# Which matmuls of two fused transformer blocks carry an order edge inside the attentions

## The chip, the cores and the metric

The kernel runs on one core of one Trainium2 chip. The metric is device time in microseconds (us), first instruction to last, as the median of three executions. The core's engines are called PE (TensorE matmul), PEld (its weight load, which overlaps PE), DVE (VectorE), ACT (ScalarE), POOL (GpSimd) and SP (SyncE, which issues most of the DMAs).

## What is computed

Two blocks follow each other on 1024 positions of width 1024, with 256 context positions beside them. The first block has two layers. Each projects its normed input to 28 tiles of 128 columns and mixes them in four ways: a short convolution, a grouped-query attention (GQA, 4 heads of 64 on 2 key heads), a gated scan (HGRN) and a Fourier mix.

```
def hybrid_layer(h, hc, ...):
    shift, scale, gate = jnp.split((c_act @ w_mod + b_mod)[:, None, :], 3, axis=-1)
    lat = split_cols((rms_norm(h, norm_g) * (1.0 + scale) + shift) @ w_in)
    att_l, att_c = gqa_branch(lat[4], lat[5], lat[6], cx[4], cx[5], cx[6], q_g, k_g, cos, sin, need_ctx)
    hg_l, hg_c = hgrn_branch(...)
    y_conv, y_four, g_att, g_hg = mix_stream(lat, conv_w)
    y = jnp.concatenate([y_conv, att_l * g_att, hg_l * g_hg, y_four], axis=-1) @ w_out
    h_new = h + gate * y
```

The second block has a latent attention (MLA, 16 heads), a state-space scan (SSD) and a gated feed-forward net. Everything is float32; a product of two float32 operands is made of three matmuls on a high and a low part.

## The kernel before

The kernel is written engine by engine, but not in the order in which the engines run it. Each instruction is traced once, in program order, and a scheduler then sets each engine's order: among the instructions whose inputs its own timing has ready, an engine takes the one that was traced first. So an instruction that is ready early can be taken ahead of others that were traced before it and still wait. An **order edge** from A to B on one engine costs no semaphore; it only tells the scheduler that B stands behind A.

Two streams are woven into each other. The foreground is a mixer (GQA, HGRN, MLA, SSD). The background, `self.lane`, holds the projections: `project` (L375: three matmuls per weight tile, `mm<-xh,wh`, `mm<-xl,wh`, `mm<-xh,wl`, into the three `mm` buffers of PSUM), the spill of each result to DRAM (`sp`), and rows of the modulation (L315, eight matmuls a row). `self.dense(us)` traces some microseconds of the lane at that place in the foreground, so that PE has something to do while the foreground waits for other engines.

The GQA of a layer (`gqa`) works in two halves, one per pair of heads. Each half begins with a prelude: load the queries (`qx`), square sums on PE (L243), their roots on DVE, a spread of the roots by PE transposes (L260), the rotation by `rope` on DVE, the split into high and low parts (`qa`), and the maxima of the first block of scores (matmul L643, reduction L490, transposes L497). Then come the steps: for each block of 512 or 256 queries, `weigh` makes the scores of a key tile (L656 and L657), their exponential (L529) and later the weighted values (L551); the maxima of the next block (`beside`) and the transposes that end the block before (`weigh_end`, L574 and L581) are traced within these steps, and so is `self.dense(wait)`. Scores, maxima and transposes share the three `t` buffers of PSUM.

In the kernel before, `weigh` opens `with self.behind(self.last):` around the whole loop over the keys (from L525), around the rest of `beside` (L547) and around the weighted values (L550). `behind` is `issue_after`: every PE instruction traced inside, by whatever it calls, gets an edge behind `self.last`, the transposes of the block's own maxima. That holds for the scores and for the projections that `dense` traces there. After the GQA follows the HGRN; each of its blocks of 512 positions has eight levels (L865, with operands made on DVE and ACT, and two `copy_predicated` L870 a level), and `dense` traces projections between the levels too, which carry no edge.

Of the kernel before, what the change touches and what calls it, by code (L numbers as in the profile page):

```python
# [15 lines left out]
AF = mybir.ActivationFunctionType  # L16
# [5 lines left out]
P = 128  # L22
# [67 lines left out]
class Kern:  # L90
# [391 lines left out]
    def put_max(self, row, nq, widths, scores):  # L482
# [4 lines left out]
        m = self.tmp("sm", (P, 4, 4), bufs=3)[:, :nq, :k]  # L487
# [8 lines left out]
        for a in range(nq):  # L496
            self.last = self.PE.transpose(t[:, a * P:(a + 1) * P], r[:, a], self.ident)  # L497
        self.S.activation(row, t, AF.Copy)

    def weigh(self, pool, out, keys, n, scores, v, beside, pieces, steps):  # L500
# [23 lines left out]
        done, left = 0, pieces + 1 if beside else 0  # L524
        with self.behind(self.last):  # L525
            for i, j in enumerate(keys):
                s = scores(j)
                e = self.ctmp(pool, "e", (P, 512), ebufs)[:, :n]
                S.activation(e, s, AF.Exp)  # L529
                count(i, e)  # L530
                es.append(e)
                self.dense(wait)
                if i == tail:
                    self.weigh_end()
                while done < left and done * (len(keys) - ahead) < (i + 1) * pieces:
                    done += 1
                    next(beside, None)
            while done < left:
                done += 1
                next(beside, None)  # L540
            self.weigh_end()

        self.last = self.scored
        for i, (j, e) in enumerate(zip(keys, es)):
            h = 64 * (i % 2)
            if i == min(4, len(keys)):
                with self.behind(self.last):  # L547
                    for _ in beside or ():
                        pass
            with self.behind(self.last):  # L550
                self.last = PE.matmul(o[h:h + 64], v(j), e, start=i < 2, stop=i >= len(keys) - 2)  # L551
        for _ in beside or ():
# [6 lines left out]
    def behind(self, ins):  # L559

        return self.tc.issue_after(ins.ins) if ins is not None else nullcontext()

    def weigh_end(self):
# [9 lines left out]
        for a in range(nq):  # L573
            PE.transpose(t[:, a * P:(a + 1) * P], total[:, a * P:(a + 1) * P], self.ident)  # L574
        r = self.tmp("sl", (P, 4), bufs=3)[:, :nq]
# [4 lines left out]
        for a in range(nq):  # L580
            PE.transpose(b[:, a * P:(a + 1) * P], r[:, a:a + 1].to_broadcast([P, P]), self.ident)  # L581
        u = self.tmp("nt")[0:64, :n]
# [46 lines left out]
    def gqa(self, pool, layer, src, need_ctx, y):  # L629
# [7 lines left out]
        def maxima(i, t0, m, h):  # L637
            cols = ALL if t0 < T else CTX

            def scores(a, c):  # L640
                c0, w = cols[c]
                s = self.psum("t")[:, :w]
                self.PE.matmul(s, qs[i][h][:, t0 + a * P:t0 + (a + 1) * P], ks[i][0][:, c0:c0 + w])  # L643
                return s
# [7 lines left out]
        def weigh(i, t0, m, h, b, beside, pieces):  # L652
            def scores(j):
                s = self.psum("t")[:, :m]
                cs = slice(j * P, (j + 1) * P)
                self.PE.matmul(s, ks[i][0][:, cs], qs[i][h][:, t0:t0 + m], start=True, stop=False)  # L656
                self.scored = self.PE.matmul(s, ks[i][1][:, cs], b[:, :m], start=False, stop=True)  # L657
                return s
# [700 lines left out]
    def mla(self, pool, more, kv, done, beside, y):  # L1359
# [39 lines left out]
        def maxima(p, h, t0, m):  # L1399
            def scores(a, c):  # L1400
                c0, w = ALL[c]
                s = self.psum()[:, :w]
                PE.matmul(s, qt[h][:, 0, t0 + a * P:t0 + (a + 1) * P], kt[h][:, 0, c0:c0 + w])  # L1403
                return s
# [3 lines left out]
        def weigh(p, h, t0, m, beside):  # L1408
            def scores(j):
                s = self.psum("t")[:, :m]  # L1410
                kh, kl = (kt[h][:, a, j * P:(j + 1) * P] for a in range(2))
                qh, ql = (qt[h][:, a, t0:t0 + m] for a in range(2))
                PE.matmul(s, kh, qh, start=True, stop=False)  # L1413
                PE.matmul(s, kh, ql, start=False, stop=False)  # L1414
# [698 lines left out]
```

## Time and profile before

| | us |
|---|---|
| median of the runs | 4070.14 |
| lowest and highest of 3 | 4065.42, 4072.88 |
| the profiled execution | 4065.49 |
| its span in the trace | 4063.6 |
| PE busy | 3739.2 (92%) |
| DVE, ACT, POOL busy | 2292.6, 1574.5, 1525.7 |

The span is what the trace shows from the first to the last instruction; 1.9 us lie around it. Matmuls are pipelined, so a matmul's own duration in the trace is longer than the distance from it to the next one. The page also gives the TensorE clock that was granted: full is 2.4 GHz, and half is 1.2 GHz. A table of stretches gives, for each, the busy time of each engine with its count of instructions, the granted clock (1.00 or 0.50 or a mean of the two), the share of the DMA engines and GB/s.

### The profile page before, as it was taken

What the parts mean: (1) busy time and instruction counts of PE and PEld (TensorE: products, weight loads), DVE (VectorE), ACT (ScalarE), POOL (GpSimd) and SP (SyncE); (2) the same over time, 40 slices, a digit from 0 to 9 for tenths busy, and PEclk for the clock granted to TensorE, in tenths of its full rate; (3) what the DMA queues carried; (4) which work ended last, traced back from release to release, by engine and by line L of the source; (5) the groups of instructions that cost most, each with busy time, mean ns of one, the idle gap of its engine ahead of it and who ended that gap; (6) DMA issues with size and microseconds to landing.
All of it is one profiled execution on the core that took longest, in us unless ns stands there. A gap on an engine that the chain in (4) does not pass through costs nothing.

```text
span 4063.6 us, 54946 instructions
## 1 busy us (share of the span) xinstructions
PE 3739.2 (92%) x19642; PEld 2879.9 (71%) x19642; DVE 2292.6 (56%) x4017; ACT 1574.5 (39%) x2851; POOL 1525.7 (38%) x1321
## 2 busy tenths in 40 slices
PE   7978999988979988987999987999999989999998
PEld 4755677767756667666767765666667979988986
DVE  5244486756245487678766776666664474424321
ACT  4223433335323445354434253444443343333332
POOL 2223311026314311255122133556665444445443
PEclk8988999999989999989999999999999999999999
DMA  6531222256532311264344567452223463333232
GB/s 213 166 101 62 88 84 80 89 182 187 187 118 65 109 65 62 78 201 141 130 151 148 184 192 217 108 149 64 51 53 122 156 197 95 98 111 124 92 115 83
DMA packets 274054, 499.54 MB, mean 123 GB/s; under 512 B 31122, under 2 KB 76978, under 8 KB 270772
## 3 DMA queue, kind: packets, MB, share of 16 engines
q1 hardware_dynamic: 269780, 467.06, 36.2%
q0 software_dynamic: 4000, 28.97, 3.0%
q8 instruction: 155, 2.54, 0.3%
q14 instruction: 119, 0.97, 0.1%
HBM read 376.70 MB, written 119.21 MB: 122 GB/s over the span
## 4 chain that ended last, share of the span: by engine, by line
PE 38%; DVE 11%; DMA 3%; issue 2%; ACT 2%; POOL 1%; SPq 0%; DVEq 0%; ACTq 0%; POOLq 0%
PE mm L207 22%; PE mm L375 5%; PE o L551 3%; DVE sm L490 3%; DVE sp L1218 2%; PE mm L1403 1%; PE t L1642 1%; PE o L1620 1%; DVE eb L519 1%; PE t L1577 1%; PE t L1415 1%; PE t L1414 1%; PE t L1413 0%; ACT sw L1610 0%; DVE sp L1215 0%
## 5 line engine op out<-in xcount | busy, mean ns | idle before, releaser
L198 POOL TENSOR_TENSOR wl<-wr,wh 128x512 fp32r<-128x512 f32 (+1 forms) x630 | 849.7, 1355 | 1540.7 <-ACT wh L197 1458.6
L375 PE MATMUL mm<-xh,wh 128*128 128x512 f32 (+1 forms) x1704 | 661.8, 389 | 16.6 <-ACT mrow L323 6.5
L375 PE MATMUL mm<-xh,wl 128*128 128x512 f32 (+1 forms) x1704 | 648.2, 381 | 1.5 <-POOL wl L198 1.5
L375 PE MATMUL mm<-xl,wh 128*128 128x512 f32 (+1 forms) x1704 | 646.7, 380 | 3.0 <-POOL xl L354 1.5
L197 ACT ACTIVATE wh<-wr 128x512 fp32r<-128x512 f32 (+1 forms) x630 | 386.7, 619 | 667.3 <-PE mm L207 253.3
L375 PEld LDWEIGHTS mm<-xh,wh 128*128 128x128 f32 x1704 | 328.5, 193 | 90.5 <-issue 10.5
L529 ACT ACTIVATE e<-t 128x512 f32<-128x512 f32 (+1 forms) x488 | 286.7, 594 | 257.8 <-PE t L1415 122.4
L522 POOL TENSOR_TENSOR ea<-ea,e 128x512 f32<-128x512 f32 x240 | 327.5, 1365 | 134.6 <-ACT e L529 124.7
L375 PEld LDWEIGHTS mm<-xl,wh 128*128 128x128 f32 x1704 | 328.1, 193 | 65.4 <-issue 4.8
L375 PEld LDWEIGHTS mm<-xh,wl 128*128 128x128 f32 x1704 | 328.2, 193 | 65.1 <-issue 6.0
L207 PE MATMUL mm<-fxh,wh 128*128 128x512 f32 (+2 forms) x1056 | 338.6, 322 | 3.2 <-ACT fxh L1794 2.1
L207 PE MATMUL mm<-fxl,wh 128*128 128x512 f32 (+2 forms) x1056 | 337.9, 320 | 1.6 <-DVE fxl L1795 1.6
L207 PE MATMUL mm<-fxh,wl 128*128 128x512 f32 (+2 forms) x1056 | 338.9, 321 | 0.0
L490 DVE TENSOR_REDUCE sm<-mm 128x1 f32<-128x512 f32 (+1 forms) x384 | 207.1, 589 | 14.2 <-PE mm L1403 14.0
L207 PEld LDWEIGHTS mm<-fxl,wh 128*128 128x128 f32 x1056 | 200.3, 190 | 19.0 <-DVE fxl L1795 2.9
L207 PEld LDWEIGHTS mm<-fxh,wh 128*128 128x128 f32 x1056 | 199.9, 190 | 18.8 <-ACT fxh L1794 2.6
L207 PEld LDWEIGHTS mm<-fxh,wl 128*128 128x128 f32 x1056 | 200.3, 190 | 15.2
L519 POOL TENSOR_TENSOR ea<-e 128x512 f32<-128x512 f32 (+1 forms) x52 | 65.3, 1255 | 307.2 <-ACT e L529 300.2
L551 PE MATMUL o<-e,v 128*64 128x512 f32 x640 | 155.5, 602 | 0.0
L375 PE MATMUL mm<-yh,wh 128*128 128x512 f32 (+1 forms) x320 | 124.5, 398 | 26.4 <-ACT yh L994 20.0
L1832 DVE TENSOR_SCALAR fc<-gs,vecs 128x512 f32<-128x512 f32 x44 | 54.8, 1245 | 163.9 <-ACT gs L1828 163.7
L584 DVE TENSOR_TENSOR nt<-o,nt 64x512 f32<-64x512 f32 (+1 forms) x52 | 34.4, 661 | 194.0 <-ACT nt L583 193.8
(466 smaller groups left out, 7890.1 us busy)
## 6 DMA issues: line engine op xcount, KB each, us to landing
mr<-w_mod SPq DMA_DIRECT2D x192, 256.0 KB, 5.2
wr<-w_in SPq DMA_DIRECT2D x190, 256.0 KB, 2.9
wr<-w_up SPq DMA_DIRECT2D x176, 256.0 KB, 2.7
wr<-w_out SPq DMA_DIRECT2D x144, 256.0 KB, 3.2
wr<-w_down SPq DMA_DIRECT2D x80, 256.0 KB, 2.6
q<-qd POOLq DMA_DIRECT2D x16, 768.0 KB, 6.1
rope<-rope SPq DMA_DIRECT2D x20, 512.0 KB, 4.3
k<-kd POOLq DMA_DIRECT2D x16, 640.0 KB, 7.3
```

The lines of the kernel that those rows point to most:

```text
L197: self.S.activation(hi, raw, AF.Copy)
L198: self.G.tensor_tensor(lo, raw, f32(hi), op=ALU.subtract)
L207: self.PE.matmul(out, a, b, start=i == 0, stop=i == n - 1)
L375: self.PE.matmul(ps, a, b, start=at + i == 0, stop=at == k_tiles - 1 and i == 2)
L490: V.tensor_reduce(m[:, a, c:c + 1], scores(a, c), axis=AX.X, op=ALU.max, negate=True)
L519: E.tensor_tensor(total, sums[E][0], e, op=ALU.add)
L522: E.tensor_tensor(sums[E][0], sums[E][0], e, op=ALU.add)
L529: S.activation(e, s, AF.Exp)
L551: self.last = PE.matmul(o[h:h + 64], v(j), e, start=i < 2, stop=i >= len(keys) - 2)
L1218: V.scalar_tensor_tensor(c, u[:, s0 + a:s0 + a + n], cw[:, a:a + 1], c, op0=ALU.mult, op1=ALU.add)
L1403: PE.matmul(s, qt[h][:, 0, t0 + a * P:t0 + (a + 1) * P], kt[h][:, 0, c0:c0 + w])
L1832: V.tensor_scalar(c, gs[:, o:o + 512], w[:, 0:1], b, op0=ALU.mult, op1=ALU.add)
```

## The change

`behind` no longer opens a block: it takes one instruction and gives that one an order edge behind `self.last`. It is called on the first matmul of each score (L643, L656, and L1403, L1413 in the MLA), on the weighted values (L551) and on the transposes of the attention (L497, L574, L581). What `dense` traces within the steps carries no edge any more.

```
     def behind(self, ins):
-        return self.tc.issue_after(ins.ins) if ins is not None else nullcontext()
+        if self.last is not None:
+            how = mybir.DependencyInfo(mybir.DependencyClass.NoSync, mybir.DependencyReason.DATA)
+            self.tc.add_manual_dep(ins.ins, self.last.ins.name, how, reason="order")
+        return ins
...
         for a in range(nq):
-            self.last = self.PE.transpose(t[:, a * P:(a + 1) * P], r[:, a], self.ident)
+            self.last = self.behind(self.PE.transpose(t[:, a * P:(a + 1) * P], r[:, a], self.ident))
...
-        with self.behind(self.last):
-            for i, j in enumerate(keys):
-                s = scores(j)
...
-                self.dense(wait)
+        for i, j in enumerate(keys):
+            s = scores(j)
...
+            self.dense(wait)
...
             if i == min(4, len(keys)):
-                with self.behind(self.last):
-                    for _ in beside or ():
-                        pass
-            with self.behind(self.last):
-                self.last = PE.matmul(o[h:h + 64], v(j), e, start=i < 2, stop=i >= len(keys) - 2)
+                for _ in beside or ():
+                    pass
+            self.last = self.behind(PE.matmul(o[h:h + 64], v(j), e, start=i < 2, stop=i >= len(keys) - 2))
...
-                self.PE.matmul(s, qs[i][h][:, t0 + a * P:t0 + (a + 1) * P], ks[i][0][:, c0:c0 + w])
+                self.behind(self.PE.matmul(s, qs[i][h][:, t0 + a * P:t0 + (a + 1) * P], ks[i][0][:, c0:c0 + w]))
```

The same wrap stands around the transposes of `weigh_end` and the first matmul of the other score functions.

What it does to the order is seen at three places. The instructions are the same ones on every engine; on PE, the rows differ from the square sums of layer 0's first GQA prelude to that layer's HGRN, and from layer 1's GQA to the first matmuls of that layer's output projection. In the MLA and behind it PE's order is unchanged.

The first place is PE in the first prelude of layer 0's GQA (L243 square sums, L260 spread of the roots, L643 maxima, L497 transposes of the maxima, L656 first score). Before, nothing stands between them:

```order
L243 MATMUL t<-bd_70,sq 128x2 x10
L260 MATMUL t<-ident,nt 128x128 x10
L643 MATMUL t<-ka,qa 128x512 x2
...
L497 MATMUL t<-ident,sr 1x128 x4
L656 MATMUL t<-qa,ka 128x512
```

The same place with the change, from the second group of square sums to the first spread:

```order
L243 MATMUL t<-bd_70,sq 128x2 x4
L375 MATMUL mm<-xh,wh 128x256
L375 MATMUL mm<-xl,wh 128x256
L375 MATMUL mm<-xh,wl 128x256
L243 MATMUL t<-bd_70,sq 128x2 x2
...
L315 MATMUL mm<-mr,mact 32x512 x8
L375 MATMUL mm<-xh,wh 128x512
L375 MATMUL mm<-xl,wh 128x512
L260 MATMUL t<-ident,nt 128x128 x4
L375 MATMUL mm<-xh,wl 128x512
```

Projections that stood within the steps now stand between the links of the prelude.

The second place is PE in the first HGRN block of layer 0 (L865 is a level's scores). Before, projections stand between one level and the next:

```order
L865 MATMUL t<-hq,hw 128x128 x8
L375 MATMUL mm<-xh,wh 128x512
L375 MATMUL mm<-xl,wh 128x512
L375 MATMUL mm<-xh,wl 128x512
...
L865 MATMUL t<-hw 128x128 x8
```

With the change the eight levels follow each other, and so do the block's outputs (L885, L888):

```order
L865 MATMUL t<-hq,hw 128x128 x8
L865 MATMUL t<-hw 128x128 x56
L315 MATMUL mm<-mr,mact 32x512
L885 MATMUL t<-sc,hv 64x128
```

The matmuls that stood there have moved to earlier places.

The third place is SP, behind the load of the first queries (`q_0`); `rope` is the rotation table that the prelude's DVE work reads, `mr` and `wr` are raw weights. A piece of the difference:

```order
 L136 DMA qx_1771<-q0_0_1307 128x1280
-L136 DMA rope_1899<-rope1 128x2x512
-L136 DMA rope_2889<-rope1 128x2x512
-L136 DMA qx_2766<-kr_0_1559 64x1280 x2
 L139 DMA hi0_0_1906<-sp_2135 128x512
...
 L136 DMA mr_2409<-w_mod 128x512
+L136 DMA rope_1899<-rope1 128x2x512
 L136 DMA mr_2411<-w_mod 128x512
```

The `rope` load now stands behind a spill of the lane and behind five loads of modulation weights.

## Rows read from the trace of the kernel before

**Rows 1.** The page: the span, the engines' busy time, the granted clock in 40 slices.
```profile
span 4063.6 us, 54946 instructions
...
PE 3739.2 (92%) x19642; PEld 2879.9 (71%) x19642; DVE 2292.6 (56%) x4017; ACT 1574.5 (39%) x2851; POOL 1525.7 (38%) x1321
...
PEclk8988999999989999989999999999999999999999
```
**Rows 2.** Stretches of layer 0: prelude, steps, prelude, steps, three of the HGRN.
```profile
219.00:260.70 41.70, 20.32 (x77) 14.67 (x75) 21.84 (x44) 8.04 (x11) 1.81 (x2) 0.60 0.30 88
260.70:345.80 85.10, 82.84 (x390) 50.65 (x389) 38.42 (x74) 37.66 (x66) 44.51 (x38) 0.97 0.15 48
345.80:387.00 41.20, 32.76 (x161) 24.71 (x159) 22.62 (x46) 9.83 (x16) 7.20 (x7) 0.80 0.40 126
387.00:479.00 92.00, 89.53 (x424) 57.22 (x422) 41.65 (x82) 36.68 (x67) 45.38 (x44) 0.98 0.11 31
...
531.00:562.20 31.20, 30.27 (x216) 23.41 (x215) 30.90 (x70) 8.52 (x15) 2.74 (x2) 1.00 0.09 33
...
583.70:613.70 30.00, 29.33 (x216) 23.02 (x215) 27.10 (x58) 9.92 (x17) 2.56 (x2) 1.00 0.27 92
613.70:635.50 21.80, 21.80 (x141) 16.02 (x140) 12.58 (x34) 3.46 (x7) 3.10 (x3) 1.00 0.10 33
```
**Rows 3.** Stretches of layer 1: prelude, steps, prelude, steps, then the HGRN's end.
```profile
1151.80:1192.20 40.40, 17.44 (x75) 11.39 (x74) 20.66 (x43) 7.54 (x11) 1.79 (x2) 0.59 0.42 133
1192.20:1258.80 66.60, 66.52 (x301) 43.10 (x300) 32.76 (x58) 28.96 (x49) 35.73 (x29) 0.96 0.08 26
1258.80:1300.10 41.30, 33.48 (x150) 21.58 (x148) 23.27 (x45) 10.93 (x17) 10.87 (x9) 0.83 0.34 106
1300.10:1385.30 85.20, 85.13 (x411) 54.44 (x410) 38.33 (x73) 33.65 (x62) 44.33 (x42) 0.98 0.19 59
...
1661.90:1691.20 29.30, 29.30 (x205) 22.36 (x204) 27.98 (x59) 9.53 (x16) 5.38 (x2) 1.00 0.07 28
1691.20:1704.70 13.50, 13.50 (x79) 9.59 (x79) 2.62 (x11) 3.15 (x4) 1.20 (x9) 1.00 0.13 40
1704.70:1749.50 44.80, 34.93 (x117) 23.27 (x115) 16.27 (x24) 18.54 (x34) 15.59 (x12) 0.81 0.68 215
1749.50:1798.80 49.30, 42.74 (x167) 33.33 (x167) 36.83 (x56) 26.22 (x50) 29.43 (x22) 0.86 0.65 204
```
**Rows 4.** PE's longest waits in the first prelude (219 to 260.7): us, times, longest.
```profile
PE t L243 <- ACT sq L461: 6.6, 1, 6.6
PE t L643 <- DVE qa L625: 6.0, 1, 6.0
```
**Rows 5.** Four stretches at half clock, each from a prelude into its steps.
```profile
227.60:265.10 37.50, 18.51 (x57) 13.32 (x58) 20.34 (x42) 7.82 (x10) 0.00 (x0) 0.50 0.21 63
...
377.70:391.40 13.70, 11.28 (x27) 7.41 (x28) 9.86 (x18) 3.36 (x6) 0.00 (x0) 0.50 0.34 111
1159.40:1196.90 37.50, 17.29 (x52) 12.46 (x53) 19.95 (x41) 7.58 (x10) 0.14 (x1) 0.50 0.29 95
...
1289.10:1302.80 13.70, 9.55 (x23) 5.97 (x24) 9.08 (x16) 4.14 (x6) 0.00 (x0) 0.50 0.00 0
```
**Rows 6.** Line 375 alone, 30 matmuls of 512 columns in a row (PE, PEld, clock, DMA).
```profile
1705.03:1712.00 6.97, 6.97 (x30) 5.54 (x30) 1.00 0.47 150
```
**Rows 7.** DVE by line in the first HGRN block: two groups of the lane's convolution.
```profile
L442 DVE SCALAR_TENSOR_TENSOR sp<-cu,vecs,sp 128x512 f32<-128x512 f32 x2 | 1.5, 745 | 0.0
L435 DVE TENSOR_TENSOR cu<-cu,mm 128x512 f32<-128x512 f32 x2 | 1.4, 682 | 0.0
```
**Rows 8.** Line 865 alone in the first HGRN block (PE, PEld, clock, DMA).
```profile
531.00:562.20 31.20, 11.58 (x128) 9.23 (x128) 1.00 0.09 33
```
**Rows 9.** Issues of DMAs: count, KB each, median us from issue to landing.
```profile
mr<-w_mod SPq DMA_DIRECT2D x192, 256.0 KB, 5.2
...
rope<-rope SPq DMA_DIRECT2D x20, 512.0 KB, 4.3
```

More of the change, by code (lines that the diff above doesn't have):

```diff
@@ L1 @@
-from contextlib import ExitStack, nullcontext
+from contextlib import ExitStack
 from itertools import chain
@@ L524, in weigh @@
         done, left = 0, pieces + 1 if beside else 0
-        with self.behind(self.last):
-            for i, j in enumerate(keys):
-                s = scores(j)
[L528 to L531, printed above, removed]
-                self.dense(wait)
[L533 to L538, printed above, removed]
+        for i, j in enumerate(keys):
+            s = scores(j)
+            e = self.ctmp(pool, "e", (P, 512), ebufs)[:, :n]
+            S.activation(e, s, AF.Exp)
+            count(i, e)
+            es.append(e)
+            self.dense(wait)
+            if i == tail:
+                self.weigh_end()
+            while done < left and done * (len(keys) - ahead) < (i + 1) * pieces:
                 done += 1
                 next(beside, None)
-            self.weigh_end()
+        while done < left:
+            done += 1
+            next(beside, None)
+        self.weigh_end()
         self.last = self.scored
@@ L573, in weigh_end @@
         for a in range(nq):
-            PE.transpose(t[:, a * P:(a + 1) * P], total[:, a * P:(a + 1) * P], self.ident)
+            self.behind(PE.transpose(t[:, a * P:(a + 1) * P], total[:, a * P:(a + 1) * P], self.ident))
         r = self.tmp("sl", (P, 4), bufs=3)[:, :nq]
@@ L580, in weigh_end @@
         for a in range(nq):
-            PE.transpose(b[:, a * P:(a + 1) * P], r[:, a:a + 1].to_broadcast([P, P]), self.ident)
+            self.behind(PE.transpose(b[:, a * P:(a + 1) * P], r[:, a:a + 1].to_broadcast([P, P]), self.ident))
         u = self.tmp("nt")[0:64, :n]
@@ L655, in scores @@
                 cs = slice(j * P, (j + 1) * P)
-                self.PE.matmul(s, ks[i][0][:, cs], qs[i][h][:, t0:t0 + m], start=True, stop=False)
+                self.behind(self.PE.matmul(s, ks[i][0][:, cs], qs[i][h][:, t0:t0 + m], start=True, stop=False))
                 self.scored = self.PE.matmul(s, ks[i][1][:, cs], b[:, :m], start=False, stop=True)
@@ L1402, in scores @@
                 s = self.psum()[:, :w]
-                PE.matmul(s, qt[h][:, 0, t0 + a * P:t0 + (a + 1) * P], kt[h][:, 0, c0:c0 + w])
+                self.behind(PE.matmul(s, qt[h][:, 0, t0 + a * P:t0 + (a + 1) * P], kt[h][:, 0, c0:c0 + w]))
                 return s
@@ L1412, in scores @@
                 qh, ql = (qt[h][:, a, t0:t0 + m] for a in range(2))
-                PE.matmul(s, kh, qh, start=True, stop=False)
+                self.behind(PE.matmul(s, kh, qh, start=True, stop=False))
                 PE.matmul(s, kh, ql, start=False, stop=False)
```

## The prediction

> **What bounds the kernel now.** The page comes first: PE is busy 3739.2 of 4063.6 us, no other engine over 57%, and the granted clock is under its full level in three of 40 slices [rows 1]. So PE bounds the kernel, and what can be won is PE's idle time and its time at half clock. Both have to be looked for in the stretches that the change touches, so the next view cuts the trace at the borders of the GQA and the HGRN. In layer 0's first prelude PE is busy 20.32 of 41.70 us, in its second 32.76 of 41.20 [rows 2]; in layer 1's two, 17.44 of 40.40 and 33.48 of 41.30 [rows 3]. DVE isn't full there either (20.66 to 23.27 us). The waits name the cause: a chain of square sums, roots, rotation and split that runs from engine to engine, with PE's longest waits on ACT's squares (6.6 us) and on DVE's `qa` (6.0 us) [rows 4]. Four stretches, of 37.5, 13.7, 37.5 and 13.7 us, ran at granted clock 0.50, the lower level of 1.2 GHz; each follows idle time in a prelude and reaches 2.7 to 4.7 us into the steps [rows 5].
>
> The steps are the opposite. PE is busy 66.52 of 66.60 us, 85.13 of 85.20, 82.84 of 85.10, and POOL, the fullest of the rest, 35.73, 44.33, 44.51 [rows 2, 3]. The first HGRN block has two full engines: PE 30.27 and DVE 30.90 of 31.20 us [rows 2].
>
> A measurement of this kernel can tell about 0.2%, 8 us, from no change.
>
> **The change part by part.** Without edges the projections that are traced in the steps may run as soon as their operands are there, so they go into the preludes. I count them from the two orders, in matmuls of 512 columns (two of 256 are one). A row of 30 of them took 6.97 us, 0.232 us each [rows 6].
>
> *Into the preludes.* They gain 117, 39.5, 120 and 41 matmuls: 317.5 x 0.232 = 73.7 us of work. One row of L315 in each layer moves in as well and leaves a place behind it where PE is as full: nothing. The idle time is 21.4 + 8.4 + 23.0 + 7.8 = 60.6 us. If the work fills it, PE pays 73.7 and gets 60.6 back. It won't fit exactly: the scheduler places matmuls by its own timing, in groups of three and on three `mm` buffers. I let a fifth, 12 us, stay idle; the ends are none and all of it.
>
> *The clock.* With PE kept busy, the lower clock has no idle time to follow. PE was busy 18.51 + 11.28 + 17.29 + 9.55 = 56.6 us at it [rows 5]; at the upper level this takes half, so 28.3 us is the most. A part was not paced by PE's clock but by operands from DVE: I take 25. The low end is nothing, if the clock falls as before.
>
> *Out of the steps.* Their four stretches lose 19.5, 35, 23 and 41 matmuls, 118.5 x 0.232 = 27.5 us. PE is nearly full there and POOL has half its time free, so most of this is time. But scores, maxima and transposes share three `t` buffers, and without projections between them a score waits for the exponential of the one before. I take 23, between 0 and 27.5.
>
> *Out of the HGRN and behind it.* The other 199 matmuls, 46.2 us, leave places that the projections filled until now. In layer 0, 75 leave the first block (17.4 us). DVE was busy for 30.90 of its 31.20 us and keeps its levels, so this is worth nothing, except that the lane's own convolution on DVE may leave too (1.5 + 1.4 us [rows 7]); I take 0. The second block loses 17 (3.9 us), with DVE at 27.10 of 30.00: at most 2.9. The stretch behind it loses 9, with PE full: 2.1. One matmul more is nothing. Together 5, between 0 and 23.7, which is all 102 of the layer. In layer 1, 5 and 11 matmuls leave long stretches in which PE sets the pace: 1.2 and 2.6 us. The last block loses 30, with DVE at 27.98 of 29.30: 1.3. Behind it 21 leave a stretch with PE full: 4.9. The last two lose 30, but PE is idle there for 9.9 and 6.6 us as it is [rows 3]: 0. Together 10, between 0 and 22.5.
>
> *A new price.* The block whose matmuls have all gone leaves PE with 11.58 us of work in 31.2 [rows 8]. So little may let the clock fall, as it did in the preludes, and the lower clock then reaches into the next full stretch. Behind the preludes this tail was 2.7 to 4.7 us, so some 2.2 us are lost each time. I count two places (this block and the last of layer 1), 4.5 us; the ends are 0 and 4.5 + 11.6 (rival three).
>
> *SP.* The rotation table's load now stands behind a spill and five loads of `mr` of 256 KB, which land 5.2 us after their issue; the table's own load takes 4.3 us [rows 9]. I count nothing: with the projections ahead, PE has other work while DVE waits for it. The end above is rival two.
>
> *The MLA* has its edges rewritten too, but PE's order there is the same: nothing.
>
> The sum: 73.7 - 60.6 + 12 - 25 - 23 - 5 - 10 + 4.5 = -33.4 us. The profiled execution took 4065.49 us, so the same execution would take 4032.1. The median of the runs is 4.65 us above it: **4037 us**. With every term at its best the sum is 73.7 - 60.6 - 28.3 - 27.5 - 23.7 - 22.5 = -88.9 us; I don't believe that DVE's full block gets shorter, nor both buffers and clock perfect.
>
> One rule speaks against the term of the steps. The steps' rows have PE full by its matmuls, but its weight loads fill only 43.10 of 66.60 us and 54.44 of 85.20 [rows 3], where a row of projections fills 5.54 of 6.97 [rows 6]. The Trainium skill, Perfetto Trace Analysis, section "Identifying the Most-Contended Engine", holds that busy matmuls are not a good measure of how close TensorE is to its limit, since they are pipelined, and that the busy share of the weight loads is the better one. By it the steps have PE time to spare, their 23 us would shrink towards nothing, and the forecast would be 4060. I stay with the row of matmuls, because scores and values need other weights than projections, and a lower share of weight loads doesn't show a wait.
>
> **The rivals.** *One: the places that the matmuls leave were not paid for by PE.* Then steps and HGRN both stay as long as they are, behind `t` buffers and DVE, and 23 + 15 us go: 4037 + 38 = 4075 us, no change that can be told. For it: the weight loads' share, and DVE's full block. Against it: the steps leave PE 0.07 to 0.08 us idle in two of four stretches, so nothing was waited for there. If only the steps give nothing, it is 4060, still faster.
>
> *Two, slower: the preludes wait for the table.* The rotation on DVE needs it, the maxima need the rotation, and the first score needs the maxima. If SP's queue (a spill that must wait for its result, then five loads) brings the table later than the hoisted matmuls last, PE idles behind them, and the preludes grow by what was put in. With idle time x left in the preludes instead of 12 and only 15 us saved by the clock, the sum is x - 35.4; it is slower by over 8 us from x = 43 on, and at the old 60.6 it is +25: 4095 us. For it: the loads' 5.2 and 4.3 us and the queries' chain, which has waits of 6 us already. Against it: the DMA engines are busy for only 0.30 to 0.42 of the four preludes [rows 2, 3], so that the five loads need not add up, and layer 0's first prelude has 117 x 0.232 = 27.1 us of new projections with which to fill the time.
>
> *Three: the emptied HGRN block runs at half clock.* Its levels go from PE to DVE and back, so doubling the 11.58 us could lengthen the block by up to as much: 4037 + 11.6 = 4049 us. In the two longest rows at the lower clock PE was busy for under half of the stretch (18.51 and 17.29 of 37.5 us), and 11.58 of 31.2 is less; the other two rows, busier, say that more can fall too [rows 5]. The Trainium skill, TensorE: Matmul & The Clock Gate, section "Part 1: The HAM clock gate", has half rate as the default and lets sustained activity alone release it; by that rule this block would fall, the preludes would rise. The preludes' rows agree with it, and no row yet shows a block of levels alone.
>
> *Four: that the change doesn't do what it says* is excluded for the order, which shows the projections moved. Whether they can start there depends on weights that have landed and been split in time. If they haven't, PE waits on them: that is a part of the 12 us and, at worst, of rival two.
>
> **How the numbers follow.** The forecast with its bounds, and with only the steps or only the clock failing, has 0.72. Rival three, inside the range, has 0.10. Rival one has 0.10, rival two 0.08. The range begins at 4006, where the idle fifth is filled, the clock gives 28.3, the steps 27.5 and the HGRN a third of the 31 us that it could still give (4037 - 12 - 3.3 - 4.5 - 10.4); it ends at 4064, just above the case of steps that give nothing. Rival one, rival two and the far best lie outside: about 0.2. Faster by over 8 us: 0.72 + 0.10 and a little of rival one, 0.83; within it 0.09; slower 0.08.
>
> **What would show it.** Right: PE over 90% busy and clock 1.00 in the four preludes, each not over 10 us longer; the steps shorter by 5, 8, 5 and 8 us; the first HGRN block still at some 31 us, DVE full and PE under half. The term of the steps is wrong if they stay within 2 us and `t` waits appear in front of the scores. The forecast falls if PE still idles 40 us or more in the preludes with DVE's rotation waiting on the `rope` load (rival two), or if the first HGRN block grows at clock 0.50 (rival three).

## The result

| | before | with the change |
|---|---|---|
| median of the runs, us | 4070.68 (4 runs) | 4021.03 (4 runs, 4015.74 to 4021.80) |
| ratio | | 0.9877, 95% interval 0.9860 to 0.9894 |
| span of the profiled execution | 4063.6 | 4019.0 |

The change is faster by 1.2%, 50 us. The forecast was 4037 us in a range of 4006 to 4064: right in its sign and its range, 16 us too slow.

The page of the changed kernel, with the rows that answer to [rows 1]: span, busy time of each engine, granted clock in 40 slices.

```profile
span 4019.0 us, 54960 instructions
...
PE 3723.7 (93%) x19642; PEld 2874.2 (72%) x19642; DVE 2288.2 (57%) x4017; ACT 1576.0 (39%) x2851; POOL 1520.3 (38%) x1321
...
PEclk8999989989999999898999989999999999999999
```

PE's busy time fell by 15.5 us, the span by 44.6: most of what went was idle time. The places show in the stretches, cut at the same instructions as in [rows 2]. Layer 0 with the change (stretch, its length, then busy time and count of PE, PEld, DVE, ACT, POOL, granted clock, DMA share, GB/s): prelude, steps, prelude, steps, the first HGRN block.

```profile
219.10:262.10 43.00, 42.06 (x233) 33.89 (x232) 23.98 (x46) 12.42 (x19) 6.98 (x6) 1.00 0.58 181
262.10:340.60 78.50, 78.40 (x375) 45.72 (x373) 38.86 (x75) 37.59 (x66) 44.61 (x38) 1.00 0.18 54
340.60:378.10 37.50, 36.37 (x205) 28.21 (x203) 23.32 (x47) 9.44 (x16) 7.09 (x7) 1.00 0.42 138
378.10:456.80 78.70, 78.59 (x377) 48.20 (x374) 41.08 (x81) 34.64 (x64) 43.84 (x42) 1.00 0.10 29
508.10:537.90 29.80, 17.16 (x132) 13.87 (x131) 28.24 (x67) 8.43 (x15) 0.00 (x0) 0.66 0.09 31
```

Layer 1 with the change, the stretches that answer to [rows 3]:

```profile
1123.90:1169.00 45.10, 42.77 (x232) 31.99 (x230) 24.49 (x46) 12.07 (x19) 6.91 (x6) 1.00 0.64 207
1169.00:1228.60 59.60, 59.47 (x279) 36.80 (x277) 31.64 (x58) 28.12 (x48) 34.90 (x28) 1.00 0.11 34
1228.60:1268.20 39.60, 38.08 (x208) 27.35 (x207) 25.97 (x47) 11.89 (x19) 12.56 (x11) 1.00 0.35 115
1268.20:1343.90 75.70, 74.84 (x354) 44.34 (x351) 38.26 (x72) 31.76 (x60) 44.23 (x42) 1.00 0.24 75
1612.80:1640.70 27.90, 23.59 (x174) 18.49 (x173) 27.76 (x59) 10.50 (x19) 4.14 (x3) 0.93 0.21 68
1640.70:1660.20 19.50, 15.25 (x57) 9.84 (x58) 3.11 (x12) 3.94 (x7) 4.50 (x12) 0.50 0.30 94
1660.20:1699.50 39.30, 27.78 (x99) 19.29 (x99) 15.29 (x23) 17.90 (x32) 13.20 (x10) 0.82 0.65 195
1699.50:1745.10 45.60, 37.93 (x155) 29.47 (x156) 37.40 (x56) 24.21 (x45) 23.82 (x19) 0.93 0.65 201
```

Three things are to be seen. The four preludes are as long as before (43.0 + 37.5 + 45.1 + 39.6 = 165.2 us against 164.6) and hold some 155 (first) and 50 (second) more PE instructions each, at clock 1.00. All four steps are shorter, 292.5 us against 328.9. And the first HGRN block has PE busy for 17.16 of 29.8 us at clock 0.66, with DVE nearly full, at much the same length.

PE's long waits in the first prelude [rows 4] are gone; one short one is left there:

```profile
PE t L260 <- DVE nt L255: 0.9, 1, 0.9
```

and DVE's wait for the rotation table there, the one of rival two, is as small (in the other three preludes it is at most 1.8 us):

```profile
DVE nt L477 <- DMA rope<-rope: 0.8, 1, 0.8
```

By stretch the account is: preludes +0.6, steps -36.4, the HGRN of layer 0 with what leads to it (479.0 to 635.5 before, 456.8 to 605.7 now) -7.6, that of layer 1 up to 1798.8 (now 1745.1) -12.3: together -55.7. Between the layers +1.9 us, and behind 1798.8 +9.1, where PE's order is unchanged. Of that last, 7 us lie at the start of the MLA, in one stretch of 385.1 us that takes 376.9 to 380.3 in the eleven other profiles with PE's same order there. Whether the other executions of the change have these 7 us isn't shown; three of the four are within 1 us of the profiled one. The layers scatter too: a trial below (edges on the values alone) has the change's order up to the MLA and ends layer 1 at 1738.8 instead of 1745.1 us, so that some 6 us between two single traces tell nothing. The medians, 50 us apart, lie between 44.6 and 55.7.

### The profile page after: what moved, and what is told of

It is laid out like the page before. It is cut to its first block, busy times and chain, and to the rows that moved or that the text cites. A ratio compares the mean times of both kernels' runs of the same rounds, so it can differ in the third digit from the quotient of the medians.

```text
span 4019.0 us, 54960 instructions
## 1 busy us (share of the span) xinstructions
PE 3723.7 (93%) x19642; PEld 2874.2 (72%) x19642; DVE 2288.2 (57%) x4017; ACT 1576.0 (39%) x2851; POOL 1520.3 (38%) x1321
## 3 DMA queue, kind: packets, MB, share of 16 engines
q1 hardware_dynamic: 269780, 467.06, 36.9%
## 4 chain that ended last, share of the span: by engine, by line
PE 38%; DVE 11%; DMA 4%; ACT 2%; issue 2%; POOL 1%; SPq 0%; DVEq 0%; ACTq 0%; POOLq 0%
PE mm L207 23%; PE mm L375 5%; PE o L548 3%; DVE sm L490 3%; DVE sp L1218 2%; PE mm L1403 1%; PE t L1642 1%; PE o L1620 1%; DVE eb L519 1%; DMA vd<-qp 1%; PE t L1577 1%; PE t L1415 1%; PE t L1414 1%; POOL wl L198 1%; DMA xt<-xtok 1%
## 5 line engine op out<-in xcount | busy, mean ns | idle before, releaser
L1832 DVE TENSOR_SCALAR fc<-gs,vecs 128x512 f32<-128x512 f32 x44 | 54.8, 1246 | 164.8 <-ACT gs L1828 164.6
L490 DVE TENSOR_REDUCE sm<-t 128x1 f32<-128x512 f32 (+1 forms) x200 | 111.9, 588 | 47.5 <-PE t L643 45.9
```

The lines of the kernel that those rows point to most:

```text
L490: V.tensor_reduce(m[:, a, c:c + 1], scores(a, c), axis=AX.X, op=ALU.max, negate=True)
L1832: V.tensor_scalar(c, gs[:, o:o + 512], w[:, 0:1], b, op0=ALU.mult, op1=ALU.add)
```

## The experiments

Twelve kernels ran; ratios are to the kernel before on the same chip.

### Edges on the projections alone are the whole difference

A kernel with the change in which only `self.dense(wait)` in `weigh` is put behind `self.last` again has the order of the kernel before, on every engine and in every row. So nothing else in the diff has an effect on this program, and the three trials that follow vary that edge.

### The change in layer 0 only

```
+            if self.hold:
+                with self.tc.issue_after(self.last.ins):
+                    self.dense(wait)
+            else:
+                self.dense(wait)
```

`self.hold` is set in layer 1 and not in layer 0.

> The change, but in layer 1 the projections traced in the steps carry the edge again; PE's order in layer 1 is then that of before. Theory (each layer's gain is its own preludes, steps and HGRN): the two traces differ by 29.9 us between layer 0's first prelude and the end of its HGRN, so 4070.7 - 30 = 4041 us (4036 to 4046), and layer 1's stretches are within 1 us of before, its two first rows at half clock (37.5 and 13.7 us) back. Rival (the gain depends on both layers, or on the MLA's start behind them): outside 4036 to 4046, or layer 1's stretches changed.

Measured: 4044.1 us, ratio 0.9928 (0.9914 to 0.9942), 29 us, within the theory. Layer 0's first prelude and layer 1's, with its steps:

```profile
218.50:261.80 43.30, 42.28 (x234) 34.02 (x232) 24.09 (x46) 12.54 (x19) 6.95 (x6) 1.00 0.59 180
1128.50:1169.10 40.60, 19.11 (x75) 11.79 (x74) 20.72 (x43) 7.56 (x11) 1.79 (x2) 0.59 0.43 132
1169.10:1235.30 66.20, 66.11 (x301) 42.83 (x300) 32.76 (x58) 28.98 (x49) 35.78 (x29) 0.97 0.08 27
```

Layer 0 reads as with the change, the GQA of layer 1 as before it (PE busy for under half of the prelude, clock 0.59). Layer 1's HGRN took 2.6 us more before its blocks and 3.1 us more in them than in the kernel before, in the same order, which is scatter again and not the 1 us that was expected. The 29 us here leave 21 of the 50 to layer 1, for which the rows have 25.8; layer 1 alone was not run.

### Each half of the attention alone

The same edge, now with `self.hold = i == 0` (the change in the second half only) and `self.hold = i == 1` (in the first half only).

> The change in the second half of each layer's GQA only: the projections traced in the first half's steps carry the edge. PE's order up to the second preludes is that of before; these then hold 110.5 and 104 projections of 512 columns instead of 67.5 and 52, their steps 78 and 69 instead of 120 and 114, and the HGRN is as before but for one matmul. Theory (a prelude's idle time is recovered whatever the other prelude does): 95 x 0.232 = 22.0 us put into the second preludes, 16.2 of idle time and 5 to 10 of half clock saved there, 87 x 0.232 = 20.2 out of the steps: 20 to 25 us faster than before. Rival (the second prelude's idle time is too short to pay): 0 to 10 us faster.

Measured: 4045.71 us, ratio 0.9935 (0.9922 to 0.9947), 26.5 us: the theory, just over its end. The second preludes and their steps account for 16.2 us of it in the trace (86.0 us instead of 82.5, and 157.5 instead of 177.2).

> The change in the first half of each layer's GQA only. The first preludes hold 142.5 and 127 projections as with the change, the first steps 39 and 18 (69 and 63 with the change, 88.5 and 86 before), the second preludes none (67.5 and 52 before), everything behind is that of before. Theory (PE sets the steps' time, the chain sets the preludes'): the first steps shorten by (49.5 + 68) x 0.232 = 27.3 us and by 4.6 of clock, the first preludes grow by 6, the second preludes stay at 41 us with PE idle for most of it: 26 us faster than before (20 to 30). Rival (the steps have a floor in POOL's sums, 44.5 and 35.7 us of 85.1 and 66.6, or in waits for exponentials, above the 57.8 and 50.8 us that are left): PE idle in the first steps and under 15 us faster.

Measured: 4062.26 us, ratio 0.9974 (0.9964 to 0.9983), 11 us. The rival holds. The two halves don't add up to the whole, since the first takes what the second prelude held. First prelude, its steps and the second prelude, of layer 0 and of layer 1:

```profile
221.30:266.40 45.10, 43.82 (x233) 35.26 (x231) 23.62 (x45) 12.52 (x19) 6.94 (x6) 0.96 0.55 172
266.40:346.40 80.00, 75.55 (x346) 42.38 (x343) 39.43 (x75) 36.73 (x65) 43.67 (x37) 0.96 0.17 50
346.40:381.70 35.30, 14.29 (x48) 9.84 (x47) 21.12 (x43) 6.21 (x9) 2.34 (x3) 0.57 0.10 35
1145.30:1191.80 46.50, 44.17 (x232) 33.19 (x229) 24.59 (x46) 11.88 (x19) 6.92 (x6) 0.96 0.63 200
1191.80:1251.30 59.50, 52.45 (x222) 27.71 (x221) 30.79 (x57) 26.36 (x45) 32.41 (x26) 1.00 0.05 16
1251.30:1288.20 36.90, 19.09 (x74) 10.99 (x72) 22.28 (x43) 9.10 (x13) 9.57 (x8) 0.65 0.10 33
```

Here the steps hold 39 and 18 projections; with the change it was 69 and 63. They take 80.0 and 59.5 us against 78.5 and 59.6: 75 projections fewer, 17.4 us of PE work, bought nothing. PE is now idle for 4.5 and 7.0 us of them, and 6.8 us of layer 0's steps ran at half clock, where all ran at full clock with the change. PE's waits in layer 1's steps say on what (lines stand five further down in this kernel: L661 is the score L656, L648 the maxima's L643, L586 the transposes L581):

```profile
PE t L586 <- DVE sl L583: 3.1, 3, 1.1
PE t L661 <- ACT e L529: 2.0, 8, 0.3
PE t L648 <- ACT e L529: 0.9, 2, 0.5
```

The last two are the `t` buffers: a score or a maximum waits for the exponential that frees one. The first is not: the block's ending transposes wait for the reciprocals that they spread (`sl`). In layer 0's steps it is 3.0 us on `sl` and only 0.6 on exponentials. POOL's 43.67 and 32.41 us are not the limit. So the steps have a floor near 78 to 80 and 60 us, and the change takes away projections just down to it. That is luck of its amounts, not of its principle. The second prelude, without any projection, took 35.3 and 36.9 us, 5.9 and 4.4 less than before: what was in it there was not quite free, though it was in idle time.

### Dummy matmuls in the preludes

The kernel before, with this behind each group of square sums and each spread in the two first preludes; `ident` times `ident` is in no result:

```
+    def warm(self, ins, n):
...
+        ps = self.psum("o")
...
+        for _ in range(n):
+            w = self.PE.matmul(ps[:, :P], self.ident, self.ident)
+            self.tc.add_manual_dep(w.ins, ins.ins.name, how, reason="order")
...
+        self.warm(at, 12)
```

> The kernel before with nothing moved; behind each group of square sums and each spread of the two first preludes, 12 matmuls of 128 columns that nobody reads keep PE busy. It tells the clock's share from that of the moved work. Theory (idle time filled by useful work is the gain, the clock adds the rest): the two half-clock stretches of 37.5 us shrink or go, the heads of the steps save 4.4/2 + 4.7/2 = 4.6 us, and at most another 9 us of PE work on the chain runs faster: 4057 to 4066 us. Rival (the clock alone carries the gain of the preludes): 25 us or more saved, 4046 us or less. If the dummies delay the chain: above 4071.

Measured: 4079.18 us, ratio 1.0018 (1.0010 to 1.0027). Theory and rival both missed: it is 7 us slower, the third case that was named, in which the dummies delay the chain. First prelude and the head of its steps, layer 0 and layer 1:

```profile
218.50:266.80 48.30, 35.39 (x219) 30.73 (x218) 21.66 (x43) 8.13 (x11) 1.81 (x2) 0.82 0.27 77
266.80:272.00 5.20, 5.20 (x17) 4.20 (x16) 1.29 (x2) 2.80 (x4) 0.00 (x0) 0.62 0.00 0
1157.40:1200.80 43.40, 27.60 (x171) 22.18 (x169) 20.75 (x43) 7.51 (x11) 1.79 (x2) 0.74 0.40 124
1200.80:1206.00 5.20, 5.20 (x15) 4.12 (x14) 1.71 (x3) 3.06 (x4) 0.66 (x1) 0.50 0.00 0
```

PE was busier and its mean clock higher (0.82 and 0.74 against 0.60 and 0.59), but the heads of the steps still ran mostly at the lower level, and the preludes grew by 6.6 and 3.0 us: a dozen matmuls behind a spread stand in front of the next one (144 dummies, 18.7 us of PE, in layer 0's prelude). The projections of the change, 27 us of them in the same prelude, cost 1.3. That speaks for work in a prelude standing where the chain waits; it doesn't follow what the clock alone is worth, since it did not stay up. That share is left open by experiment.

### Dummy matmuls in the emptied HGRN blocks

The same helper, with the change, behind each level of layer 0's first block and layer 1's last, and behind their outputs.

> The change, with matmuls that nobody reads behind each level of layer 0's first HGRN block and of layer 1's last (10 of 128 columns a level, 12 behind the outputs), to hold the clock that fell there. Theory (the fall costs what follows the block: 19.5 us now against 13.5 before in layer 1, with 21 projections fewer): clock 1.00 in both blocks, the stretch behind layer 1's last block at 13 us or less, 4021 - 6 = 4015 us (4010 to 4018). Rival (block and tail are set by DVE and the chain, not by PE's clock): 4019 to 4024 us though the clock is 1.00. Delay by the dummies: above 4024.

Measured: 4018.68 us, ratio 0.9867 (0.9853 to 0.9882): from the change's 0.9877 it can't be told, and it lies between the theory's end and the rival's beginning. Layer 0's block, then layer 1's block and three stretches behind it:

```profile
509.60:540.10 30.50, 30.40 (x289) 28.13 (x288) 28.78 (x68) 7.66 (x14) 0.00 (x0) 0.98 0.11 39
1620.10:1649.30 29.20, 29.19 (x290) 26.88 (x289) 27.35 (x59) 7.97 (x14) 0.00 (x0) 1.00 0.09 29
1649.30:1664.00 14.70, 14.70 (x97) 11.22 (x97) 1.93 (x10) 3.14 (x4) 0.00 (x0) 1.00 0.00 1
1664.00:1706.60 42.60, 33.68 (x118) 22.48 (x116) 17.19 (x23) 18.27 (x34) 16.82 (x21) 0.84 0.71 225
1706.60:1757.20 50.60, 43.12 (x167) 34.07 (x168) 37.48 (x56) 26.28 (x49) 28.63 (x23) 0.87 0.63 200
```

The clock stayed at or near its upper level in both blocks, and the stretch behind layer 1's block went from 19.5 to 14.7 us, where the theory had 13 or less. The two stretches behind that took 42.6 and 50.6 instead of 39.3 and 45.6: the three together 107.9 against 104.4. But the trial moved more than the clock. PE's counts there are 97, 118 and 167, where the change has 57, 99 and 155: layer 1's block holds none of the 45 projections that it holds with the change; 15 of them stand in the stretch behind it and 30 in the next one, and 12 other matmuls of that one went to the last. So these rows don't tell what the clock is worth at the end of layer 1. Nor does the equal time: in the trace layer 1 ends 12.1 us later than with the change, and what follows in PE's same order is 11.4 us shorter, 6.3 of it in the MLA's stretch of 385.1 us. With the clock up, layer 0's block is no shorter either (30.5 against 29.8, DVE 28.78); that agrees with DVE as its limit, but doesn't show it, since the dummies fill PE there.

### No edges at all, and edges on the values alone

```
     def behind(self, ins):
-        if self.last is not None:
+        if False:
```

> The change, but behind() adds no edge at all, in GQA and MLA: the attentions' own matmuls are free too. The order then has 39, 46, 31 and 41 projections in the four steps instead of 69, 85, 63 and 73, and 60 instead of 0 in layer 0's first HGRN block. Theory (the steps are PE-bound down to that, the emptied HGRN has room): up to 15 us faster than the change in the two layers, 4006 us, plus what the MLA makes of its own order. Rival (with so few projections the steps wait for exponentials, sums and t buffers, and own matmuls out of order delay them): steps as long as with the change, PE idle in them, 4021 us or more; if the MLA needs its edges, 4030 us or more.

Measured: 4074.55 us, ratio 1.0005 (0.9993 to 1.0016): the whole gain is gone, as in the last case that was named (4030 us or more), but PE is not idle in the steps. Layer 0's two steps without edges:

```profile
261.90:342.80 80.90, 79.94 (x332) 40.80 (x329) 40.64 (x75) 36.39 (x64) 43.91 (x39) 1.00 0.08 23
379.70:466.50 86.80, 85.78 (x349) 42.74 (x347) 41.41 (x82) 33.79 (x62) 41.69 (x42) 1.00 0.16 49
```

They hold fewer matmuls than with the change (332 for 375, 349 for 377) and take longer, with PE busy all the time. The weighted values alone (line 548, 551 in the kernel before: length, PE, PEld, clock, DMA) show why; here without edges, one of the steps and the sum of the four:

```profile
261.90:342.80 80.90, 31.22 (x88) 6.81 (x88) 1.00 0.08 23
...
sum 309.80, PE 121.22 PEld 25.57; mean PE 30.31 PEld 6.39
```

and with the change:

```profile
262.10:340.60 78.50, 20.96 (x88) 5.79 (x88) 1.00 0.18 54
...
sum 292.50, PE 74.54 PEld 20.45; mean PE 18.64 PEld 5.11
```

A value is a matmul on half of the array's columns, 128*64, whose turns alternate between the two halves; the trace has two matmuls for each value, one behind the other. In a row, neighbours on the two halves overlap: the 88 took 0.24 us each, though one lasts 584 ns. Without edges, 69 of the 94 rows of values in the four steps are a single value between other matmuls; with the change none is. From the timelines (start, length, then the matmuls and their number), without edges:

```profile
266.15 0.39 PE L643 MATMUL t<-ka,qa 128*128 128x512 f32 x1
266.47 1.07 PE L548 MATMUL o<-e,vt 128*64 128x512 f32 x2
267.47 0.39 PE L643 MATMUL t<-ka,qa 128*128 128x256 f32 x1
```

and with the change:

```profile
274.05 1.94 PE L548 MATMUL o<-e,vt 128*64 128x512 f32 x8
275.92 0.60 PE L497 MATMUL t<-ident,sr 128*1 128x128 f32 x4
```

A single value takes 1.00 us to the start of the next matmul, four in a row 1.87 us. A smaller part of this is the step from one form to the other: the value starts 0.32 us behind the start of a full-width matmul, where projections follow each other by 0.232 us [rows 6]. Without edges the matmuls of the values took 0.35 to 0.40 us each (121.22 us for 322 over the four steps, 74.54 for 316 with the change). That is 46.7 us more (43.3 if each is counted up to the start of the matmul behind it), against 133 projections fewer (290 to 157), 30.9 us: a net of 15.8, where the steps are 17.3 us longer. Here a stretch with PE busy for 98.8% held less work than the same one with the change; the weight loads, 40.80 against 45.72 us, told it. The Trainium skill, TensorEngine Tiling (Array Packing), section "Tiling Modes", lists 128x64 as two tiles that are independent of each other; the rows agree, with 0.24 us a matmul in a row against 0.35. The MLA lost nearly as much again as the layers: layer 1 ended 26.2 us later than with the change, and the MLA's two stretches were 391.9 and 1247.0 us, against 385.1 and 1234.3 (378.0 and 1234.1 before the change).

The last trial of this group keeps the edge on the values and takes it from scores, maxima and transposes.

> The change, with an edge on the weighted values alone; scores, maxima and transposes carry none. In the GQA of both layers every engine's order is that of the change; PE's order differs only within the MLA. Theory (only the values need the edge, since two of them run side by side when they follow each other: without any edge their busy time in the four steps was 121.2 us against 74.5): the same as the change within 5 us, and the MLA's stretch within 5 us too. Rival (the MLA needs the edges on scores and transposes): 10 us slower or more than the change, all of it in the MLA.

Measured: 4044.66 us, ratio 0.9935 (0.9921 to 0.9948). In the GQA the order is that of the change, and so are the steps (78.6, 78.7, 59.7 and 75.7 us); the rival holds in the MLA. Its two stretches with the change and, below, with edges on the values alone:

```profile
2387.10:2772.20 385.10, 349.99 (x1675) 235.34 (x1675) 238.04 (x433) 156.37 (x286) 191.21 (x161) 0.98 0.50 134
2772.20:4006.50 1234.30, 1198.82 (x6664) 1005.17 (x6663) 532.67 (x805) 470.87 (x833) 617.85 (x523) 0.99 0.36 107
```

```profile
2380.90:2772.40 391.50, 360.20 (x1676) 238.30 (x1676) 235.72 (x434) 155.29 (x287) 191.83 (x161) 0.97 0.49 132
2772.40:4024.90 1252.50, 1219.37 (x6663) 1012.76 (x6662) 531.30 (x805) 468.82 (x833) 617.80 (x523) 0.98 0.36 106
```

Together 24.6 us longer, as much as the medians differ (23.6). So the GQA needs the edge on its values and the MLA on its other matmuls too.

### Projections held back in the HGRN

```
+            if lv and True:
+                with self.tc.issue_after(at.ins):
+                    self.dense(HGRN_WAIT[3])
...
+                    at = PE.matmul(ss[h][:, cs], kh[r, cs], qh[r, cs])
```

> The change, and in each HGRN block the projections traced at a level carry an edge behind the matmuls of the level before. The blocks then hold as many projections as before (75 a block); what they give up is 102 and 116 in the stretches between the GQA's end and the first block (138 to 36, 193 to 77). Theory (there PE sets the pace: 45.94 of 51.3 us and 68.44 of 79.0 busy): these two stretches shorten by up to 15 us each, the blocks grow by 1 to 3: 10 to 25 us faster than the change. Rival (loads, DVE and ACT set these stretches, so the projections were free there and in the blocks): the stretches stay within 4 us of the change, PE idle in them, and the time is 0 to 8 us above the change.

Measured: 4042.18 us, ratio 0.9925 (0.9912 to 0.9937): 20 us slower than the change, past the rival's end, though PE idles in the stretches that the rival named. The stretches of layer 0 and layer 1 between the GQA and the first block, and then layer 1's first blocks:

```profile
456.40:508.10 51.70, 25.66 (x145) 21.49 (x143) 31.26 (x54) 27.35 (x34) 2.56 (x2) 0.70 0.35 116
...
1351.20:1429.00 77.80, 37.70 (x224) 30.25 (x222) 50.52 (x89) 46.23 (x55) 5.45 (x4) 0.74 0.17 52
1429.00:1630.50 201.50, 182.53 (x1069) 139.92 (x1068) 149.18 (x297) 81.12 (x114) 30.78 (x20) 0.94 0.19 62
```

The first two, with 102 and 116 projections fewer, took 51.7 and 77.8 us; with the change it was 51.3 and 79.0. PE is idle for half of them, so projections ride there for nothing, in layer 1 nearly so. Of the price, 11.6 us were in layer 1's first blocks: 201.5 us instead of 189.9, with 35 projections more. Here work belongs into the GQA's preludes and the stretches ahead of the HGRN's blocks, not into the blocks.

### How much is traced in the steps

`GQA_STEPS` sets 0.5 us of the lane a key. With the change it no longer sets the steps' fill (the order up to the GQA's end holds as much), but it shifts what comes behind.

> The change with 0.4 instead of 0.5 us of the lane traced at each key of the GQA's steps. Up to the GQA's end PE's order holds as many projections as with the change; the first HGRN block of layer 0 then keeps 56.5 of its own (none with the change) and the blocks behind it hold fewer (32, 37 instead of 58, 63). Theory (that block has PE time for nothing: 17.16 of 29.8 us busy with the change): 13 us of work go into its shade and come off stretches behind it that are PE-full (19.70 of 19.7, 86.59 of 94.3 us): 4 to 10 us faster than the change. Rival (the blocks behind are set by DVE as well, so work that leaves them is worth nothing): within 3 us of the change.

Measured with 0.4: 4020.30 us, ratio 0.9879 (0.9866 to 0.9893), the rival: the same as the change.

> The change with 0.6 instead of 0.5 us of the lane traced at each key of the GQA's steps; the first HGRN block of layer 0 then holds 20 projections, the next ones 69.5 and 75 (58 and 63 with the change). Theory (what counts is which stretches have PE time to spare; preludes and steps are as with the change): the first block takes 4.6 us of work for nothing, the next ones 5.4 us more, not for nothing: 0 to 4 us faster than the change. Rival (blocks set by DVE): the same, within 3 us; more than 4 us either way speaks against both.

Measured with 0.6: 4003.94 us, ratio 0.9839 (0.9826 to 0.9853), 16 us faster than the change: more than either had. The first block isn't where it comes from:

```profile
512.00:546.00 34.00, 26.16 (x173) 19.86 (x172) 28.46 (x68) 8.68 (x15) 0.00 (x0) 0.75 0.31 100
```

It is 4.2 us longer, though DVE is busy for as long as with the change (28.46 us): with projections back in it, the lower clock does cost time there (from 536 to 540 us PE is full at clock 0.50 and DVE busy for 1.35 us). The gain stands between the layers, 508.4 us instead of 518.2 with 27 PE instructions fewer and 8.6 us less of PE's time, and in the end of layer 1 (14.5 + 37.6 + 45.1 = 97.2 us instead of 104.4); but traces with one and the same order between the layers took 513.7 to 521.0 us there. Layer 1 ends 9.8 us earlier in all. Of 9.2 us behind it, 6.9 are in the MLA's first stretch, 378.2 us here as in the other kernels.

> The change with 0.65 us of the lane traced at each key of the GQA's steps (0.5 with the change, 0.6 before this run). Layer 0's first HGRN block holds 42 projections, layer 1's second one 35 instead of 59. Theory (what is left to win is the first block's idle PE): within 5 us of 0.6, 3999 to 4009 us. Rival (0.6 was a lucky order, and any shift of the lane moves the time by 10 us or more): outside of that.

Measured with 0.65: 4022.39 us, ratio 0.9881 (0.9867 to 0.9894): the same as with 0.5. The rival holds: 0.6 is a lucky order, and no direction was found in which more is better.

> The kernel before, edges as they were, with 0.6 instead of 0.5 us of the lane traced at each key of the GQA's steps. It tells whether the 16 us that 0.6 gave beside the change belong to the amount alone. Theory (with the edges, more projections at each key go into steps that PE already fills): no faster than before, 4065 to 4080 us. Rival (the amount is worth its 16 us with or without the edges): 4050 to 4058 us.

Measured: 4068.79 us, ratio 0.9993 (0.9983 to 1.0003). The amount alone does nothing; the 16 us need the change. The change with 0.6 is the fastest version of this study.

## Why the prediction was right, and where it was short

**The preludes** came out as forecast in mechanism. Their terms in the sum were +73.7, -60.6, +12 and -25 us, +0.1 together; the rows give +0.6. But 12 us left idle was too much: PE's idle time in the four is 5.9 us. And the clock's 25 us included half of the four tails that [rows 5] show in the steps (4.4, 4.4, 4.7 and 2.7 us), 8 us that are to be looked for there. With these two the preludes' own clock share comes to 73.7 - 60.6 + 5.9 - 0.6 = 18.4 us, which with the tails makes 26: the size was right. It is what is left of a sum of rows; the dummies did not show it alone. The bound of 28.3 us was too low, since the kernel before has two more stretches at half clock, in the second preludes and with PE full:

```profile
357.30:364.10 6.80, 6.80 (x23) 5.84 (x22) 2.03 (x10) 0.32 (x1) 0.00 (x0) 0.50 0.00 0
1275.50:1278.90 3.40, 3.40 (x9) 2.63 (x8) 1.45 (x7) 0.00 (x0) 0.00 (x0) 0.50 0.87 225
```

With them PE was busy at half clock for 66.8 us, and 33.4 is the most. (The clock's row in [rows 1] is under 90% in five slices, not in three.)

**The steps** are the term of the sum that was mis-sized. It said 23 us out of at most 27.5, and the steps lost 36.4, of which 8 are the clock's tails; 28.4 stand for the projections, the bound itself. The discount for the three `t` buffers was the wrong step: the traces show no wait on them in any of the four steps, and PE is busy 78.40 of 78.50 us in the first. The mechanism exists: in the trial with the first halves alone a further 17.4 us bought nothing, with PE idle on those buffers and, for longer, on the reciprocals of the sums, and the clock down for 6.8 us. The steps were PE-paced down to the amount that the change leaves, and stop near there. The rule of the Trainium skill that stood against this term (Perfetto Trace Analysis, section "Identifying the Most-Contended Engine"), by which the forecast would have been 4060, did not hold for [rows 3]: the steps shortened by all of the work. It did hold for the run without edges, where busy time was no measure of work. Neither view alone told which; the count of matmuls by their pace did.

**HGRN and behind it** gave 19.9 us, where 15 less 4.5 for the clock was forecast. Layer 0's first block went as said: DVE at 28.24 of 29.8 us, length -1.4 us, clock 0.66; the 2.7 us that left DVE are about what the lane's convolution [rows 7] was said to take along. In layer 1 the long row of blocks gave 6.6 us (2.6 forecast), a part of which may be scatter. The end of layer 1, from its last block on, came out by luck: 4.6 us shorter, where 1.3 and 4.9 less half of 4.5 were counted. The stretch behind the last block, for which 4.9 were counted as won, cost 6.0: the fall of the clock was no tail of 2.2 us, but a stretch at 0.50 from 1636.8 to 1674.3 us. And the last two stretches, where nothing was counted, gave 5.5 and 3.7 for the 30 matmuls (7.0 us) that left them: PE's idle time there, 9.9 and 6.6 us, was not used up instead, it is 11.5 and 7.7 now, so these places had been paid for by PE. The run with dummies, which has 30 projections back there, took 42.6 and 50.6 us (44.8 and 49.3 before). What the fall of the clock cost by itself at this end, the runs don't settle.

**The rivals.** Rival one (the places that matmuls leave were not paid by PE) fell for the steps and held for the first HGRN block; and it is what awaited the next 17 us in the steps. Rival two fell: DVE waits for the table for 0.8 us, and at most 1.8. Rival three came half true, with the clock at 0.66 in the block, and cost the block nothing, since DVE is full there; 11.6 us of it didn't come. With 20 projections back in the block it did cost (34.0 us with 0.6). **The sum** was short by 5.4 (steps), 6.1 (idle time), 1.4 (clock in the preludes) and 9.4 us (HGRN and behind), 22.3 in all, from -33.4 to the -55.7 of the rows. A part is given back between and behind the layers, so that the forecast of the median is nearer than its terms; how much of that is chance isn't known.

## What to carry to other kernels

An edge that is set around a block binds what other code issues inside it; set it on the instructions whose order matters, and find out which they are by taking edges off one kind at a time. Before moving filler, count by stretch which engine sets its end: here filler was worth its full time where a chain of engines left PE idle, nothing in DVE's block or ahead of the HGRN's blocks, and it could be taken out of the steps only down to a floor that a busy PE hid. Busy time of PE doesn't say whether its matmuls run side by side; compare the time per matmul, from start to start, between two orders. And before a difference of a few us between two traces is explained, see how far two traces of one order differ.

## What was not expected

The matmuls of the weighted values took 0.24 us each in a row and 0.35 to 0.40 us each when most values stood alone, so the order alone moved 46.7 us of PE's busy time with 322 and 316 such matmuls in the four stretches. And a dozen matmuls of 128 columns behind each group of square sums and each spread lengthened a prelude by 6.6 us in which PE had been idle for 21.4: idle time in this chain couldn't be filled at any place in it.
